# A hybrid decoder layer on one core: the input projection with seven doubled Strassen products, and attention in one small PSUM bank

## The chip, the cores and the metric

The kernel runs on one core of one Trainium2 chip. The metric is the device time of one execution in microseconds (us). The engines are named as in the profile: PE (TensorE, matmuls), PEld (its weight loads, which overlap PE), DVE (VectorE), ACT (ScalarE), POOL (GpSimd) and SP (SyncE, which issues most DMAs). PE writes its results into PSUM, which the kernel uses as eight banks of 128 x 512 float32.

## The reference

One layer on 512 tokens of width 2048, all in float32:

```python
h = rmsnorm(x, attn_norm_g)
proj = h @ w_in              # 2048 -> 9216: u, v_sgu, q, k, v_att (1024 each), g_a, g_b (2048 each)
u = gelu(u); v_sgu = rmsnorm(gelu(v_sgu), sgu_norm_g)          # 8 groups of 128
y_a = u * (tril(w_s) @ v_sgu + b_s)                            # in chunks of 128 tokens
q = rmsnorm(q, q_norm_g); k = rmsnorm(k, k_norm_g)             # 8 heads of 128
z = q @ k.T * scale                                            # strictly causal
w = exp(log_sigmoid(z) + reverse_cumsum(log_sigmoid(-z)) - log_sigmoid(-z))   # stick breaking
y_b = w @ v_att
x = x + (sigmoid(g_a) * (y_a @ w_up_a) + sigmoid(g_b) * (y_b @ w_up_b)) @ w_o
hid = rmsnorm(x, ffn_norm_g) @ w_ffn_in                        # 2 x 5632
x = x + (silu(gate) * up) @ w_ffn_out
x = x + sigmoid(rmsnorm(x, ple_norm_g) @ w_ple_gate) * (p @ w_ple)
```

## The kernel before

Activations lie transposed, features on the 128 partitions and the 512 tokens along the row. Every float32 product is made of three reduced ones: a number is split into a high part (`whi` for weights, made by ACT) and a low remainder (`wlo`, made by DVE), and high x high, high x low and low x high are added in a PSUM bank. On top of it lies a Strassen scheme: an output pair (256 features x 512 tokens, class `Pair`) is built from seven products of 128 x 128 blocks of weights with 256 columns of activations, instead of eight. DVE and ACT form the sums of weight blocks before (L382, splits L363 and L366), and the sums of products after (the generators `mix` and `mix_doubled`, in lines L757 and L760).

A product comes in two forms. In the **narrow** form (`mm3`, lines L296 to L298) it is three matmuls of 256 columns, and two products share a bank, one in each half. In the **doubled** form (L701) it is one matmul of 512 columns, high weights against the high and the low activations side by side, and one of 256 columns with the low weights. A doubled product needs a bank of its own, and the two halves of that bank are added later. The argument `doubled` of a pair says how many of its seven products take this form: 5 in the input projection, 7 in w_o, the feed-forward and its output.

The input projection has 36 pairs: q, k and v of round 0, some gates, q, k and v of round 1, and so on for four rounds of two heads each, then the gated branch (units s and u). Three pairs at the start are plain; the other 33 run over all 2048 inputs in four quarters of two weight blocks each, 14 products a quarter. Twice in a quarter `tick()` advances a clock and issues work that has come due: builds of operands, and the steps of the generators started with `beside`: flips (transposes) with the norms of q, k and v, attention, gating. A `yield n` in such a generator means "go on n ticks later". The order in which an engine gets its instructions follows the program, but a step of a generator may stand later among the products, and products of the next quarter may be drawn ahead; the chains made with `in_turn` and `mark` hold the weights and the mix in their order.

Eight PSUM banks are shared: six in the pool `psm` (tile `ps`) for products, two in the pool `psa` (tile `small`). With 5 doubled products a pair of the projection takes five banks and one for the two narrow products, so all of `psa` is for the steps beside it, and they take its two banks by turns: flips (L1055), scores (stage a, L1129), running sums (stage d, L1166 and L1167), the product with v (finish, L1181) and the gating (L1240). In pairs with 7 doubled products the seventh takes a bank of `psa`, by turns too.

Of the kernel before, what the change touches and what calls it, by code (L numbers as in the profile page):

```python
# [70 lines left out]
def hybrid_layer(  # L71
# [25 lines left out]
    psa = ctx.enter_context(tc.tile_pool(name="psa", bufs=2, space=PSUM))  # L97
# [85 lines left out]

    def bank():
        return psm.tile([P, T], F32, tag="ps", name=nm("ps"))
# [54 lines left out]
    class Staged:  # L240
# [23 lines left out]
        def get(self):  # L264
            while not self.done:
                self.advance()
            return self.result

# [373 lines left out]
    class Pair:  # L642
# [329 lines left out]
    class Norm:  # L972
# [17 lines left out]
        def steps(self):  # L990
            ps = small_bank()
            for t in range(NT):
                nc.tensor.matmul(ps[:, t : t + 1], self.acc.f(t * P, (t + 1) * P), ones[:, 0:1],
                                 start=True, stop=True)
            yield
            self.mean = consts.tile([P, NT], F32, name=nm("mean"))
            nc.vector.tensor_scalar(out=self.mean, in0=ps[:, :NT], scalar1=1.0 / D, scalar2=EPS,
                                    op0=ALU.mult, op1=ALU.add)
            self.cols = consts.tile([P, NT], F32, name=nm("cols"))
            nc.gpsimd.tensor_tensor(out=self.cols, in0=self.mean, in1=expo[:, :NT], op=ALU.pow)  # L1000
            for _ in range(3):
                yield
            ps = spread(self.cols)
# [99 lines left out]
    def v_prep(o, v):  # L1103
        for h in range(2):
            yield 2
            times(v[:, h * T : (h + 1) * T], flip(o[:, h * T : (h + 1) * T]), norm1.cols)

    def attention(rnd, kT, rk, v):
# [80 lines left out]
        blocks = [(h, j) for h in range(2) for j in range(NT - 1, -1, -1)]  # L1189
        stage_a(*blocks[0])  # L1190
        yield 1
        stage_m(*blocks[0])
        yield 1
        stage_a(*blocks[1])
        for i, (h, j) in enumerate(blocks):
            ahead = blocks[i + 1 : i + 3]
            if i == NT + 1:
                finish(0)
            stage_b(j)
            yield 1  # L1200
            stage_c(j)
# [9 lines left out]
        yield 1  # L1211
        finish(1)
# [4 lines left out]
    def sgu_v(rnd, o):  # L1217

        for h in range(2):
# [7 lines left out]
            yield 2  # L1227
# [8 lines left out]
            yield 2  # L1236
            mp = small_bank()
# [32 lines left out]
    def made():  # L1270
# [54 lines left out]
    for n, ((w, i), pr) in enumerate(zip(order, made())):  # L1325
# [10 lines left out]
        elif w == "k":  # L1336
            kT, rk = o, rms_tile()
            beside(k_prep(kT, rk))
            beside(attention(i, kT, rk, a_tile("v", 1024)), 6)
        elif w == "v":  # L1340
            beside(v_prep(o, a_tile("v", 1024)))
# [263 lines left out]
```

## Time and profile before

| | |
|---|---|
| median of 3 runs | 2657.65 us (2652.71 to 2658.19) |
| profiled execution | 2652.22 us; span 2650.5 us; TensorE clock 0.999 |
| PE, PEld busy | 2635.0 us (99%), 2301.7 us (87%) |
| DVE, ACT, POOL busy | 2255.1 us (85%), 1409.0 us (53%), 451.5 us (17%) |
| matmuls | 15202 |
| loads of the projection's weights (w_in) issued | 58.8 to 780.5 us; the last finish of attention (L1181) at 589 us |
| loads of w_ffn_in issued | 1152.9 to 1996.4 us |

The page of the profile gives, for each engine, busy time and number of instructions. A row of groups reads: line, engine, operation, output <- inputs, shapes, count, then busy time and mean duration in ns, then the idle time of the engine just before and what ended it. A row of the chain or of the timeline begins with the start in us from the span's start, and the length. Matmuls overlap in the pipeline: the chain shows what each adds, the timeline how long each is under way.

### The profile page before, as it was taken

Reading aid. Unit: us, or ns where it says so; the run is one execution under the profiler, and the core shown is the slowest. Engines: PE = TensorE matmul, PEld = TensorE weight load, DVE = VectorE, ACT = ScalarE, POOL = GpSimd, SP = SyncE. Lnnn points to the kernel's source line nnn. Section 1 sums busy time; section 2 is a strip of 40 time slices with the busy share of each in tenths; the row PEclk is TensorE's granted clock in tenths of the full one; section 3 lists DMA queues with packets and bytes.
Section 4 is the critical chain, followed back from the end, with each engine's and each line's share of the span. In section 5 each row is a group of like instructions: output and inputs, shape, how many; then the busy total and the mean of one; then the engine's idle time right before and its main releaser. Section 6 shows DMA issues by size and latency. Waiting matters only on the chain.

```text
span 2650.5 us, 42355 instructions
## 1 busy us (share of the span) xinstructions
PE 2635.0 (99%) x15202; PEld 2301.7 (87%) x15202; DVE 2255.1 (85%) x3856; ACT 1409.0 (53%) x2245; POOL 451.5 (17%) x559
## 2 busy tenths in 40 slices
PE   9999999999999999999999999999999999999999
PEld 7888888889998888888888888888888888889888
DVE  8687878787887558999888888888889989989898
ACT  7756565655554335466444444444445445455543
POOL 0222223232220001101111111111110211211010
PEclk9999999999999999999999999999999999999999
DMA  6777777677775669988888788888887989988794
GB/s 209 183 195 171 194 172 192 171 192 191 175 195 186 223 224 271 254 246 212 223 213 217 197 203 203 195 212 201 202 203 225 255 227 275 225 242 254 239 269 137
DMA packets 288130, 561.46 MB, mean 212 GB/s; under 512 B 26288, under 2 KB 133552, under 8 KB 287920
## 3 DMA queue, kind: packets, MB, share of 16 engines
q1 hardware_dynamic: 225856, 440.77, 50.6%
q0 software_dynamic: 61776, 117.47, 27.8%
q8 instruction: 119, 1.95, 0.3%
q14 instruction: 91, 0.75, 0.1%
q10 hardware_dynamic: 288, 0.52, 0.1%
HBM read 507.28 MB, written 51.38 MB: 211 GB/s over the span
## 4 chain that ended last, share of the span: by engine, by line
PE 94%; DVE 3%; ACT 1%; DMA 1%; issue 1%; SPq 0%; DVEq 0%; ACTq 0%
PE ps L701 56%; PE ps L298 9%; PE ps L297 9%; PE ps L296 9%; PE small L701 6%; DVE wlo L363 1%; PE small L1181 1%; PE small L1129 1%; PE small L1055 1%; DVE parts L287 1%; DVE wholes L534 0%; DVE wholes L382 0%; PE small L1240 0%; DMA wholes<-x 0%; DMA wholes<-w_ffn_out 0%
## 5 line engine op out<-in xcount | busy, mean ns | idle before, releaser
L701 PE MATMUL ps<-parts,whi 128*128 128x512 f32 x4390 | 1470.6, 398 | 1.9 <-DVE out L806 0.8
L366 ACT ACTIVATE whi<-wholes 128x512 fp32r<-128x512 f32 (+2 forms) x934 | 873.1, 948 | 759.4 <-DVE wholes L382 308.6
L363 DVE TENSOR_TENSOR wlo<-wholes,whi 128x512 fp32r<-128x512 f32 (+2 forms) x934 | 980.8, 1086 | 78.5 <-ACT whi L366 77.6
L701 PEld LDWEIGHTS ps<-parts,wlo 128*128 128x128 f32 x4390 | 823.9, 188 | 188.0 <-DVE wlo L363 2.5
L701 PE MATMUL ps<-parts,wlo 128*128 128x256 f32 x4390 | 868.4, 279 | 1.1 <-DVE wlo L363 1.1
L701 PEld LDWEIGHTS ps<-parts,whi 128*128 128x128 f32 x4390 | 707.2, 189 | 11.3 <-issue 3.1
L297 PE MATMUL ps<-parts,whi 128*128 128x256 f32 (+1 forms) x1622 | 538.4, 332 | 1.0 <-DVE parts L287 0.9
L298 PE MATMUL ps<-parts,wlo 128*128 128x256 f32 (+1 forms) x1622 | 538.3, 333 | 1.1 <-DVE wlo L363 1.1
L296 PE MATMUL ps<-parts,whi 128*128 128x256 f32 (+1 forms) x1612 | 532.5, 332 | 1.8 <-ACT parts L286 1.4
L382 DVE TENSOR_TENSOR wholes<-wholes 128x256 f32<-128x256 f32 x820 | 346.3, 422 | 15.8 <-DVE wlo L363 0.4
L760 DVE TENSOR_TENSOR out<-out,ps 128x256 f32<-128x256 f32 x525 | 216.8, 416 | 152.2 <-ACT out L757 152.0
L297 PEld LDWEIGHTS ps<-parts,whi 128*128 128x128 f32 x1622 | 305.9, 189 | 37.9 <-DVE parts L287 2.9
L298 PEld LDWEIGHTS ps<-parts,wlo 128*128 128x128 f32 x1622 | 306.2, 189 | 30.6 <-DVE wlo L363 1.5
L296 PEld LDWEIGHTS ps<-parts,whi 128*128 128x128 f32 x1612 | 303.5, 189 | 32.2 <-ACT parts L286 2.2
L370 POOL DMA_DIRECT2D wholes<-w_ffn_in x169 | 147.6, 873 | 704.2 <-DVE wholes L382 209.7
L370 POOL DMA_DIRECT2D wholes<-w_in x132 | 117.0, 888 | 543.1 <-DMA wholes<-w_in 112.3
L701 PE MATMUL small<-parts,whi 128*128 128x512 f32 x480 | 190.2, 397 | 0.0
L757 ACT ACTIVATE out<-ps 128x256 f32<-128x256 f32 x279 | 104.7, 385 | 57.0 <-PE ps L701 52.9
L287 DVE TENSOR_TENSOR parts<-wholes,parts 128x1024 fp32r<-128x1024 f32 (+3 forms) x139 | 124.0, 904 | 12.6 <-ACT parts L286 12.5
L286 ACT ACTIVATE parts<-wholes 128x1024 fp32r<-128x1024 f32 (+3 forms) x139 | 107.8, 797 | 46.5 <-DVE wholes L534 32.4
L370 POOL DMA_DIRECT2D wholes<-w_ffn_out x64 | 55.9, 873 | 356.0 <-DMA wholes<-w_ffn_out 84.7
L1428 ACT ACTIVATE out<-out 128x512 f32<-128x512 f32 x44 | 27.9, 633 | 156.2 <-DVE out L1427 156.2
(135 smaller groups left out, 1833.6 us busy)
## 6 DMA issues: line engine op xcount, KB each, us to landing
wholes<-w_ffn_in SPq DMA_DIRECT2D x169, 384.0 KB, 5.6
wholes<-w_in SPq DMA_DIRECT2D x132, 384.0 KB, 5.0
wholes<-w_ffn_in SPq DMA_DIRECT2D x169, 256.0 KB, 4.8
wholes<-w_ffn_in POOLq DMA_DIRECT2D x169, 256.0 KB, 5.4
wholes<-w_in SPq DMA_DIRECT2D x132, 256.0 KB, 4.1
wholes<-w_in POOLq DMA_DIRECT2D x132, 256.0 KB, 5.0
wholes<-w_ffn_out SPq DMA_DIRECT2D x64, 384.0 KB, 6.0
wholes<-x SPq DMA_DIRECT2D x46, 512.0 KB, 6.1
```

The costliest lines, as they stand in the source:

```text
L286: return (nc.scalar.activation(hi, src, AF.Copy), nc.vector.tensor_tensor(out=lo, in0=src, in1=hi.bitcast(F32), op=ALU.subtract))
L287: nc.vector.tensor_tensor(out=lo, in0=src, in1=hi.bitcast(F32), op=ALU.subtract))
L296: nc.tensor.matmul(ps, sh, mh, start=start, stop=False)
L297: nc.tensor.matmul(ps, sh, ml, start=False, stop=False)
L298: return nc.tensor.matmul(ps, sl, mh, start=False, stop=stop)
L363: in_turn(nc.vector.tensor_tensor(out=self.lo[:, blocks], in0=r, in1=h.bitcast(F32), op=ALU.subtract))
L366: in_turn(nc.scalar.activation(h, r, AF.Copy))
L370: nc.gpsimd.dma_start(out=raw[:, 3:5], in_=self.src[:, 1:3], accum_op=ALU.add)
L382: in_turn(nc.vector.tensor_tensor(out=o, in0=x, in1=y, op=ALU.add))
L701: m = nc.tensor.matmul(out, l, r, start=first and k == 0, stop=last and k == 1)
L757: in_turn(nc.scalar.activation(out, x, AF.Copy, scale=scale))
L760: in_turn(nc.vector.tensor_tensor(out=out, in0=x, in1=y, op=op))
```

## The change

The pairs of the input projection get `doubled=7`. Their seventh product takes a bank, so the pool `psa` now holds one bank called `last`, for the seventh product wherever a pair has one (in the pairs with both kinds of operands and 5 doubled products, for the bank called z), and one called `small` for all the steps beside. A new generator `turn(ticks)` lets a step wait until the ticks that the step before it took are over. `until_made` makes attention wait for q, k and v, which are now made at ticks that are not known beforehand; the sums, the finish and the scores, which were issued in one tick, are now in ticks of their own.

```diff
-    psa = ctx.enter_context(tc.tile_pool(name="psa", bufs=2, space=PSUM))
+    psa = ctx.enter_context(tc.tile_pool(name="psa", bufs=1, space=PSUM))
...
+    def last_bank():
+        return psa.tile([P, T], F32, tag="last", name=nm("last"))
...
+    taken = [0]
+
+    def turn(ticks):
+
+        while clock[0] < taken[0]:
+            yield 1
+        taken[0] = clock[0] + ticks
...
-                small = "z" if self.both and self.doubled else len(PRODUCTS) - 1
-                self.banks[name] = small_bank() if name == small else bank()
+                last = "z" if self.both and self.doubled else len(PRODUCTS) - 1
+                self.banks[name] = last_bank() if name == last else bank()
...
         def steps(self):
+            taken[0] = max(taken[0], clock[0] + 1)
             ps = small_bank()
...
         for h in range(2):
-            yield 2
+            yield 2 - h
+            yield from turn(2)
             ps = flip(o[:, h * T : (h + 1) * T])
...
             yield 2
+            yield from turn(1)
             if not h:
                 y_b[i] = take(1024)
             nc.scalar.activation(y_b[i].f(h * T, (h + 1) * T), flip(q.f()), AF.Copy,
                                  scale=gcol[:, g_q : g_q + 1])
             give(q)
-
-    def k_prep(o, rk):
+            made_up.add(("q", i, h))
+
+    made_up = set()
+
+    def until_made(*what):
+        while what not in made_up:
+            yield 1
...
-            yield 2
+            yield 2 - h
+            yield from turn(1)
             times(v[:, h * T : (h + 1) * T], flip(o[:, h * T : (h + 1) * T]), norm1.cols)
+        made_up.add(("v", i))
...
+        yield from until_made("k", rnd)
+        yield from until_made("q", rnd, 0)
+        yield from turn(1)
         stage_a(*blocks[0])
         yield 1
         stage_m(*blocks[0])
         yield 1
+        yield from turn(1)
         stage_a(*blocks[1])
         for i, (h, j) in enumerate(blocks):
             ahead = blocks[i + 1 : i + 3]
-            if i == NT + 1:
-                finish(0)
             stage_b(j)
             yield 1
+            if i == NT + 1:
+                yield from until_made("v", rnd)
+                yield from turn(1)
+                finish(0)
             stage_c(j)
             if ahead:
                 stage_m(*ahead[0])
             yield 1
             if not ahead:
                 yield 1
+            yield from turn(1)
             stage_d(h, j)
+            yield 1
             if ahead[1:]:
+                yield from until_made("q", rnd, ahead[1][0])
+                yield from turn(1)
                 stage_a(*ahead[1])
-            yield 1
         yield 1
+        yield from turn(1)
         finish(1)
...
             yield pair(xs, last=i == len(srcs) - 1, home=lambda: block(*order[i]),
-                       doubled=5)
+                       doubled=7)
```

The flips of k and the two uses of the gating get a `turn` in the same way.

What PE gets, in a quiet quarter of a pair of the gated branch. Before, the fifth product is doubled and the rest is narrow (`ps_631` holds both narrow products):

```order
L701 MATMUL ps_630_6215<-parts_73,whi1_77 128x512
L701 MATMUL ps_630_6215<-parts_73,wlo1_78 128x256 x2
L701 MATMUL ps_630_6215<-parts_73,whi1_77 128x512
L296 MATMUL ps_631_6220<-parts_73,whi1_77 128x256
L297 MATMUL ps_631_6220<-parts_73,whi1_77 128x256
L298 MATMUL ps_631_6220<-parts_73,wlo1_78 128x256
```

On PE after, in the first quarter of the next pair of that branch (lines are eleven higher; `ps_674` is the first product's bank, `ps_678`, `ps_679` and `last_680` those of the fifth, sixth and seventh):

```order
L712 MATMUL ps_678_5939<-parts_73,whi1_77 128x512
L712 MATMUL ps_674_5913<-parts_73,whi0_75 128x512
L712 MATMUL ps_674_5913<-parts_73,wlo0_76 128x256
L712 MATMUL ps_679_5944<-parts_73,whi1_77 128x512
L712 MATMUL ps_679_5944<-parts_73,wlo1_78 128x256 x2
L712 MATMUL ps_679_5944<-parts_73,whi1_77 128x512
L712 MATMUL last_680_5949<-parts_73,whi1_77 128x512
L712 MATMUL last_680_5949<-parts_73,wlo1_78 128x256 x2
```

Twelve narrow matmuls of a quarter have become eight of L712, in two banks; two matmuls of the next quarter (weights `whi0`, `wlo0`) have been drawn ahead of the sixth product. Pairs with seven doubled products elsewhere show the same at their start.

On PE before, sums and scores in an attention round, in two banks (`small_600`, `small_601`); the finish ahead of them stands nine products earlier:

```order
L297 MATMUL ps_599_5801<-parts_73,whi0_75 128x256
L298 MATMUL ps_599_5801<-parts_73,wlo0_76 128x256
L1166 MATMUL small_600_5814<-parts_73,tri1_133 128x256
L1167 MATMUL small_600_5814<-parts_73,tri1_133 128x256
L1129 MATMUL small_601_5821<-wholes_74 128x512
L701 MATMUL ps_593_5761<-parts_73,whi2_79 128x512
```

On PE after, the same three uses from the end of the finish (L1207) over the sums (L1192, L1193) to the scores (L1155), now all in the one bank:

```order
L1207 MATMUL small_645_5569<-wholes_74 128x128
L712 MATMUL ps_641_5527<-parts_73,whi1_77 128x512
L712 MATMUL ps_641_5527<-parts_73,wlo1_78 128x256 x2
L712 MATMUL ps_641_5527<-parts_73,whi1_77 128x512
L1192 MATMUL small_647_5596<-parts_73,tri1_133 128x256
L1193 MATMUL small_647_5596<-parts_73,tri1_133 128x256
L712 MATMUL last_642_5532<-parts_73,whi1_77 128x512
L712 MATMUL last_642_5532<-parts_73,wlo1_78 128x256 x2
L712 MATMUL last_642_5532<-parts_73,whi1_77 128x512
L712 MATMUL ps_634_5490<-parts_73,whi0_75 128x512
L712 MATMUL ps_634_5490<-parts_73,wlo0_76 128x256 x2
L1155 MATMUL small_649_5628<-wholes_74 128x512
```

The finish has moved to two products ahead of the sums, and the scores have moved from right behind the sums to where a product and two thirds lie between (seven matmuls).

On DVE before, the end of the mix of a pair (`p5` is a scratch tile, `wholes` and `out` hold the output):

```order
L760 TENSOR_TENSOR wholes_74<-wholes_74,p5_632_6322 128x2x256
L760 TENSOR_TENSOR wholes_74<-wholes_74,ps_630_6215 128x256
L760 TENSOR_TENSOR wholes_74<-ps_631_6220,wholes_74 128x512
L382 TENSOR_TENSOR wholes_74<-wholes_74 128x256
L1250 TENSOR_TENSOR wholes_74<-wholes_74 128x1024
```

On DVE after:

```order
L771 TENSOR_TENSOR wholes_74<-wholes_74,p5_681_6035 128x2x256
L771 TENSOR_TENSOR wholes_74<-wholes_74,ps_678_5939 128x256
L771 TENSOR_TENSOR wholes_74<-ps_679_5944,wholes_74 128x256
L771 TENSOR_TENSOR wholes_74<-last_680_5949,wholes_74 128x256
L771 TENSOR_TENSOR wholes_74<-wholes_74,ps_679_5944 128x256
L771 TENSOR_TENSOR wholes_74<-wholes_74,last_680_5949 128x256
L393 TENSOR_TENSOR wholes_74<-wholes_74 128x256
L1288 TENSOR_TENSOR wholes_74<-wholes_74 128x1024
```

One operation of 512 columns has become four of 256, two for each of the two new banks.

More of the change, by code (lines that the diff above doesn't have):

```diff
@@ L1002, in steps @@
                 yield
+            taken[0] = max(taken[0], clock[0] + 2)
             ps = spread(self.cols)
@@ L1095, in q_prep, with k_prep, v_prep @@
             give(q)
-    def k_prep(o, rk):
+            made_up.add(("q", i, h))
[3 more added lines that the diff above has]
+            yield 1
+    def k_prep(o, rk, i):
         for h in range(2):
-            yield 2
+            yield 2 - h
+            yield from turn(1)
             token_rms(flip(o[:, h * T : (h + 1) * T]), rk[:, NT * h : NT * (h + 1)])
         nc.scalar.activation(o, o, AF.Copy, scale=gcol[:, g_k : g_k + 1])
-    def v_prep(o, v):
+        made_up.add(("k", i))
+    def v_prep(o, v, i):
         for h in range(2):
-            yield 2
+            yield 2 - h
+            yield from turn(1)
             times(v[:, h * T : (h + 1) * T], flip(o[:, h * T : (h + 1) * T]), norm1.cols)
+        made_up.add(("v", i))
     def attention(rnd, kT, rk, v):
@@ L1206, in attention @@
                 yield 1
+            yield from turn(1)
             stage_d(h, j)
+            yield 1
             if ahead[1:]:
+                yield from until_made("q", rnd, ahead[1][0])
+                yield from turn(1)
                 stage_a(*ahead[1])
-            yield 1
         yield 1
+        yield from turn(1)
         finish(1)
@@ L1226, in sgu_v @@
             nc.sync.dma_start(out=bb, in_=b_s[g : g + 1, :].broadcast_to([P, P]))
-            yield 2
+            yield 2 - h
+            yield from turn(2)
             gv = a_tile(("l", "w0")[rnd % 2])
@@ L1236, in sgu_v @@
             yield 2
+            yield from turn(1)
             mp = small_bank()
@@ L1337, in hybrid_layer @@
             kT, rk = o, rms_tile()
-            beside(k_prep(kT, rk))
+            beside(k_prep(kT, rk, i))
             beside(attention(i, kT, rk, a_tile("v", 1024)), 6)
         elif w == "v":
-            beside(v_prep(o, a_tile("v", 1024)))
+            beside(v_prep(o, a_tile("v", 1024), i))
         elif w == "s":
```

## The prediction, made before the changed kernel ran

> **What bounds the kernel now.** I read the page first (busy shares, chain of waits), then the waits of TensorE (PE) alone, then the chain in a quiet stretch of the input projection beside one of the feed-forward stage, and last the timeline around the attention's banks.
>
> ```profile
> PE 2635.0 (99%) x15202; PEld 2301.7 (87%) x15202; DVE 2255.1 (85%) x3856; ACT 1409.0 (53%) x2245; POOL 451.5 (17%) x559
> PE 94%; DVE 3%; ACT 1%; DMA 1%; issue 1%; SPq 0%; DVEq 0%; ACTq 0%
> wholes<-w_in SPq DMA_DIRECT2D x132, 384.0 KB, 5.0
> ```
>
> PE is busy for 99% of the span and carries 94% of the chain, so an edit counts if it changes what PE streams or makes PE wait. The third row counts the work: 132 loads of weights, four to a pair of output tiles, are the 33 pairs that the change touches.
>
> The next answer is the waits of PE between 56 and 735 us, where the attention runs beside the projection; then four stretches of time (their length, then busy time and count of PE, PEld, DVE, ACT, POOL, then clock, DMA share, GB/s).
>
> ```profile
> PE small L1129 <- ACT wholes L1078: 1.2, 3, 0.5
> ```
> ```profile
> 56.00:735.00 679.00, 677.73 (x4283) 603.45 (x4282) 549.04 (x998) 421.48 (x890) 176.19 (x240) 1.00 0.73 183
> 273.70:293.50 19.80, 19.80 (x119) 16.93 (x118) 19.01 (x39) 14.50 (x30) 8.39 (x12) 1.00 0.74 199
> 610.10:629.90 19.80, 19.80 (x131) 17.99 (x131) 15.71 (x26) 10.96 (x14) 3.47 (x4) 1.00 0.77 189
> 1440.00:1459.80 19.80, 19.80 (x116) 17.28 (x115) 17.58 (x33) 9.64 (x14) 3.46 (x4) 1.00 0.79 200
> ```
>
> PE waits 1.2 us in 679: there is almost nothing to win from waits, and all that the two small banks do today is already hidden. DVE has room on the whole (549 of 679), but not in the middle of an attention round (19.01 of 19.80).
>
> **Part 1: products 5 and 6 doubled.** Here is the chain in a quiet pair of the input projection, then in a feed-forward pair, which already has seven doubled products (start, length, what).
>
> ```profile
> 601.51 3.51 PE ps L701 x20
> 605.02 0.12 PE ps L296
> 605.14 0.12 PE ps L297
> 605.26 0.12 PE ps L298
> ...
> 606.46 3.51 PE ps L701 x20
> ...
> 621.30 3.51 PE ps L701 x20
> ```
> ```profile
> 1464.37 4.19 PE ps L701 x24
> 1468.56 0.70 PE small L701 x4
> 1469.26 4.18 PE ps L701 x24
> ...
> 1483.90 0.24 PE ps L701
> ```
>
> A quarter pair of the projection is 20 matmuls for ten doubled products (3.51 us, 0.351 each) and twelve narrow ones for four products (605.02 to 606.46, 1.44 us, 0.36 each). Four quarters take 621.30 - 601.51 = 19.79 us. The feed-forward pair has the same 56 products, all doubled, and takes 1483.90 - 1464.37 = 19.53. The change makes the one into the other: 0.26 us a pair, 33 pairs, 8.6 us less. The low bound is the price of the products alone, 0.36 - 0.351 = 0.009 for 2 x 8 x 33 = 528 products, 4.8 us; I take the pair because it includes the passages between the kinds. So the instructions removed, 528 of 15202 or 3.5%, are worth only 0.3%: a wide matmul streams the columns of the two it replaces.
>
> [...]
>
> **Part 2: the mix on DVE.** One subtraction of 512 columns goes, four of 256 come. First the projection's end of a pair, then the feed-forward's:
>
> ```profile
> 603.62 0.68 DVE L760 TENSOR_TENSOR out<-ps,out 128x512 f32<-128x512 f32 x1
> 604.23 0.88 DVE L382 TENSOR_TENSOR wholes<-wholes 128x256 f32<-128x256 f32 x2
> ```
> ```profile
> 1442.12 0.42 DVE L760 TENSOR_TENSOR out<-ps,out 128x256 f32<-128x256 f32 x1
> 1442.45 0.41 DVE L760 TENSOR_TENSOR out<-small,out 128x256 f32<-128x256 f32 x1
> 1442.79 0.41 DVE L760 TENSOR_TENSOR out<-out,ps 128x256 f32<-128x256 f32 x1
> 1443.11 0.41 DVE L760 TENSOR_TENSOR out<-out,small 128x256 f32<-128x256 f32 x1
> 1443.44 0.42 DVE L382 TENSOR_TENSOR wholes<-wholes 128x256 f32<-128x256 f32 x1
> ```
>
> From start to next start the one takes 0.61 us, the four take 1443.44 - 1442.12 = 1.32: DVE gets 0.71 us more a pair, 23 us in all. In the quiet pair that is 16.4 of 19.5, less than the 17.58 that the feed-forward carries with no stall, so it costs nothing. In the worst pair of a round it is 19.01 + 0.71 = 19.7 against 19.5: DVE is full, and 0.2 us late with what follows. The cover is the room of the pairs beside it and the weights split ahead. I price it at 0; with that cover gone it is 0.2 to 0.7 us in perhaps two pairs of each of four rounds, 1.6 to 5.6 us. ScalarE's (ACT's) four copies a pair stay.
>
> **Part 3: one bank called last, also behind the attention.** The seventh product had two banks by turns in the feed-forward, w_o, w_ffn_out; now one. PE before wrote the next one while DVE still read the old one (1443.11 + 0.41 = 1443.52):
>
> ```profile
> 1443.28 0.40 PE L701 MATMUL small<-parts,whi 128*128 128x512 f32 x1
> 1443.63 0.39 PE L701 MATMUL ps<-parts,whi 128*128 128x512 f32 x1
> ```
>
> That can't be any more. But the order now puts two matmuls of the next quarter and the sixth product ahead of it, so that it would start near 1443.63 + 0.70 = 1444.33, 0.8 us after the read. I price it at 0; were DVE later by more than 0.8 us at every boundary, some 60 pairs would pay the excess.
>
> **Part 4: attention, flips and gating through one small bank.** This is the unknown, since nothing in the trace uses one bank for all of it. A round has 26 uses (8 flips, 8 scores, 8 sums, 2 finishes), four rounds 104. Each use must now wait until ACT or DVE has read the one before. With PE first in line for 99% of the span, each such wait is lost time; and behind the waiting matmul stands every product of the projection. The timeline before, at the finish of the first half of the third round (L1181 is the finish and L1183 reads it; L1167 ends the sums and L1173 reads them):
>
> ```profile
> 422.85 0.27 DVE L1173 TENSOR_TENSOR wholes<-wholes,small 128x128 f32<-128x128 f32 x1
> 423.26 2.39 PE L1181 MATMUL small<-wholes 128*128 128x512 f32 x8
> 425.69 0.60 ACT L1183 ACTIVATE wholes<-small 128x512 f32<-128x512 f32 x1 [1.65 <-PE small L1181]
> 428.80 0.28 PE L1167 MATMUL small<-parts,tri 128*128 128x256 f32 x1
> 429.86 2.27 DVE L363 TENSOR_TENSOR wlo<-wholes,whi 128x1280 fp32r<-128x1280 f32 x2
> 432.45 0.40 DVE L1173 TENSOR_TENSOR wholes<-wholes,small 128x256 f32<-128x256 f32 x1
> ```
>
> At 423.26 PE writes a bank whose last read ended at 422.85 + 0.27 = 423.12: the order brings the use 0.14 us after the release, and PE has no idle time there. That is the row nearest to the new situation. The order of the changed kernel shows how many products now lie between two uses. At this same place they are two (0.70 us) from the finish to the sums, whose reader needs 0.04 + 0.60 us; and 1.17 us from the sums to the scores. Before, the sums ended near 429.08 and were read by 432.85, 3.77 us later, since a split of weights of 2.27 us stood ahead on DVE. If DVE is free, the read is done 0.8 us after the sums.
>
> ```profile
> L1078 ACT ACTIVATE wholes<-small,cols 128x128 f32<-128x128 f32 x32 | 9.5, 369 | 3.2 <-PE small L1055 3.2
> L1131 ACT ACTIVATE wholes<-small,rr 128x512 f32<-128x512 f32 x8 | 5.5, 689 | 5.3 <-PE small L1129 4.6 <-DVE wholes L382 0.7
> L1132 ACT ACTIVATE wholes<-small,rr 128x512 f32<-128x512 f32 x8 | 5.5, 684 | 0.9 <-DVE wholes L534 0.9
> ```
>
> The other short distances of a round, by the order: 4 products (1.40 us) after a flip of v, whose readers need 4 x 0.369 = 1.48; 4 products after scores of 512, whose readers need 0.689 + 0.684 = 1.37; and 1.63 and 1.51 us after two other sums. The rest have 2.1 to 12.8 us.
>
> Low end: every use arrives after its release, 0 us; or the 1.2 us that PE waits today goes too, since scores now start only once q is made. High end: the three short distances after sums (1.63, 1.51, 1.17) meet a read 3.8 us late, 7.1 us a round, 28 us in four rounds. I take 0.5 us a round (0.1 to 0.2 for each flip, score and finish above, the sums mostly in time), 2.0 us, near the low end, because PE came 0.14 us behind a release without waiting. The flips and their readers move later by a tick or two; nothing queues behind that, since by the order the second finish of a round lies 12.8 us of PE work ahead of the next round's first flip.
>
> **The sum.** -8.6 (products) + 0 (mix) + 0 (last bank) + 2.0 (small bank) = -6.6 us. The profiled execution took 2652.22 us (span 2650.5 and 1.7 around it), so 2645.6. It stands 5.4 us under the median of the three runs, 2657.65 (2652.71 to 2658.19); from that median the sum gives 2651.0. Two of three runs lie at the upper value, so I say 2650.
>
> **Rivals.** One: a product costs its columns and nothing else. All products stream 768 columns before and after, so the gain is about 0, and 2.0 of waits stand against it: 2654 from the own time. The row of 0.36 against 0.351 and the 19.53 us pair speak against it. [...]
>
> Two, the same time in another way: the gain is given back in waits of 3.3 to 13.9 us, 0.8 to 3.5 us a round, at the short distances or at the full pairs of DVE: 2646.9 to 2657.5 from the own time, 2652 in the middle. The 19.01 of 19.80 speaks for it, that PE today waits for no read of a bank against it.
>
> Three, slower: reads of the sums stay 3.8 us late, because they still stand behind weight splits on DVE, which now also carries 0.71 us more a pair. PE then stops in each round at the three short distances, 28 us in all, less 8.6: 2671. It decides from 3.5 us of waits a round (8.6 + 5.3 over four rounds). For it speaks the 3.77 us above, and that the order of the changed kernel still has two splits ahead of such a read on DVE; against it, that those splits may be over by then, since scores and sums come later than before.
>
> **How the numbers follow.** About 0.2% (5.3 us) is what a measurement of this kernel tells from no change. The sum's case (net gain 5.3 to 9.8 us) gets 0.57; rival one 0.06 and rival two 0.24, together 0.30 for the same; rival three 0.13. So faster 0.57, same 0.30, slower 0.13. The low end is the full 8.6 and the 1.2 from the own time, 2642.4, with a little for the runs' spread: 2641. The high end is a median of runs unchanged and a small loss of 3 us: 2661. Under the sum's case alone it is 2642 to 2652.
>
> **What would show it.** Right: PE's narrow products L296 to L298 of the projection gone, quiet pairs at 19.53 us in place of 19.79, PE at 14674 matmuls, feed-forward pairs still at 19.53. The small bank: PE's waits between 56 and 730 us name ACT and DVE readers of it and sum to about 2 us (high: 28). DVE in the worst 19.5 us stretch full, with no PE wait on wlo. Wrong: quiet pairs above 19.7 us (rival one), PE waits over 3.5 us a round behind the sums' readers or at a pair's start (rivals two, three), or feed-forward pairs above 19.53 (part 3).

## Result and the profile after

The changed kernel takes 2673.95 us, the median of 6 runs (2668.51 to 2678.19), beside 2655.47 for the kernel before on the same chip (6 runs). The ratio is 1.0069, interval 1.0055 to 1.0083: 0.7% slower, where 2650 us was forecast. The profiled execution took 2676.11 us, its span is 2674.4 us, against 2650.5 before.

The page of the changed kernel, busy shares and the chain of waits (share of the span by engine):

```profile
PE 2639.3 (99%) x14674; PEld 2274.5 (85%) x14674; DVE 2278.2 (85%) x3955; ACT 1407.6 (53%) x2245; POOL 440.0 (16%) x559
PE 79%; DVE 11%; DMA 4%; issue 2%; ACT 2%; POOL 1%; DVEq 0%; POOLq 0%; SPq 0%; ACTq 0%
```

The 528 matmuls are gone, as announced, and DVE has 23 us more. PE still reads 99% busy, which tells nothing of the loss. The second row does: PE's share of the chain fell from 94% to 79%, and DVE, DMA, ACT and POOL carry parts of it now.

PE's waits between 56 and 735 us (what PE was to run, for whom it waited; total, times, longest), where before showed 1.2 us for the scores:

```profile
PE small L1278 <- ACT wholes L1091: 6.5, 3, 2.9
PE small L1192 <- ACT wholes L1158: 4.0, 1, 4.0
PE small L1192 <- ACT parts L1182: 1.0, 3, 0.3
PE small L1207 <- ACT wholes L1158: 0.7, 2, 0.5
PE ps L712 <- DVE wlo L374: 0.2, 1, 0.2
PE ps L712 <- DVE p L771: 0.2, 1, 0.2
```

Together they are 12.6 us, where about 2 were forecast. The first four rows are matmuls into the small bank, and all four wait for ACT: L1278 is the gating product, L1192 the first matmul of a sum, L1207 the finish; L1091 scales the gating input by its power, L1158 reads scores, L1182 makes the high half of the sums' operand. DVE's splits of weights (wlo), where the prediction looked, stand in one row of 0.2 us. The window ends ahead of one gating product; with it the first row is 9.5 us in 4 waits, the longest 3.0.

The chain in the last pair of the projection (start, length, what):

```profile
788.24 0.70 PE last L712 x4
788.94 4.54 PE ps L712 x26
...
807.76 0.70 PE last L712 x4
```

From one seventh product to that of the next pair it is 807.76 - 788.24 = 19.52 us, against 19.79 before: a quiet pair does win its 0.27 us.

Where the 23.9 us of the two spans lie is seen from the start of one pair to the start of a later one (worked out from PE's matmuls in both traces; 33 pairs, and what is before and behind them):

| stretch | before, us | after, us | difference |
|---|---|---|---|
| ahead of the pairs | 84.5 | 85.2 | +0.7 |
| 7 pairs with round 0 | 156.77 | 162.19 | +5.4 |
| 6 + 6 pairs with rounds 1, 2 | 268.33 | 268.94 | +0.6 |
| 5 pairs with round 3 | 111.50 | 112.87 | +1.4 |
| 7 pairs with gating | 149.27 | 159.57 | +10.3 |
| last 2 pairs | 39.57 | 39.04 | -0.5 |
| behind the projection | 1840.6 | 1846.6 | +6.0 |

So there are three losses: the gating, the rounds, the start of the up-projection. In the places shown below, something in an engine's queue waits for a transfer or a buffer, and work that PE needs stands behind it.

**The gating.** Rows of the timeline of after, on POOL, ACT and PE (start, length, engine, line; in brackets the idle time before and what ended it):

```profile
645.89 0.89 POOL L381 DMA_DIRECT2D wholes<-w_in  x1 [4.56 <-DMA wholes<-w_in]
646.46 1.39 POOL L965 TENSOR_TENSOR rr<-ms,expo 128x4 f32<-128x4 f32 x1
647.89 1.14 ACT L1091 ACTIVATE wholes<-small,rr 128x128 f32<-128x128 f32 x4 [2.80 <-POOL rr L965]
649.08 1.16 PE L1278 MATMUL small<-wholes 128*128 128x128 f32 x8 [2.88 <-ACT wholes L1091]
```

L381 is POOL's issue of the transfer that adds one block of weights onto another. Here the load below it landed at 645.23, and the issue began at 645.89, after POOL had stood idle for 4.56 us; the power of 128x4 numbers (L965), next in POOL's queue, begins at 646.46 although DVE had its operand ready at 642.08, ACT's scaling waits 2.80 us for the power, and the gating product, with all of PE behind it, 2.88 us for the scaling. The same place before:

```profile
633.79 0.89 POOL L370 DMA_DIRECT2D wholes<-w_in  x1 [2.17 <-DVE ms L1231]
634.37 1.39 POOL L954 TENSOR_TENSOR rr<-ms,expo 128x4 f32<-128x4 f32 x1
635.79 1.14 ACT L1078 ACTIVATE wholes<-small,rr 128x128 f32<-128x128 f32 x4 [1.67 <-POOL rr L954]
636.40 1.08 PE L1240 MATMUL small<-wholes 128*128 128x128 f32 x8
```

The order was the same and PE did not wait, but the slack was small: the product began 0.61 us after the scaling did, while it was still under way. In this place the load was asked for at 639.10 and landed at 645.23 (6.1 us); before it was asked for at 630.25 and landed at 633.13 (2.9 us). In both kernels a split of weights on DVE releases the load (L374, begun at 637.59; before L363, at 628.74).

**Round 0.** The same on POOL's masks, after:

```profile
153.47 0.89 POOL L381 DMA_DIRECT2D wholes<-w_in  x1 [4.39 <-issue]
154.06 0.62 POOL L1168 TENSOR_SCALAR_AFFINE_SELECT wholes<-wholes 128x128 f32<-128x128 f32 x1
154.74 0.20 POOL L1176 MEMSET wholes<- 1x128 f32 x1
154.97 0.63 ACT L1182 ACTIVATE parts<-wholes 128x512 fp32r<-128x512 f32 x1 [4.08 <-POOL wholes L1176]
156.17 0.36 ACT L1158 ACTIVATE wholes<-small,rr 128x128 f32<-128x128 f32 x1
156.57 0.79 PE L1192 MATMUL small<-parts,tri 128*128 128x512 f32 x1 [3.99 <-ACT wholes L1158]
```

The bracket of the first row says issue, which names no releaser; the load that this issue adds onto landed at 152.43. The mask waits behind the issue on POOL, the copy L1182 for the mask on ACT, the read of the next scores (L1158) behind that copy, and PE for the read, since there is one bank: 3.99 us.

**The start of the up-projection**, ACT and PE after:

```profile
833.25 1.06 ACT L377 ACTIVATE whi<-wholes 128x1024 fp32r<-128x1024 f32 x1 [3.00 <-PE ps L308]
834.22 1.04 ACT L297 ACTIVATE parts<-wholes 128x1024 fp32r<-128x1024 f32 x1
835.31 0.73 PE L307 MATMUL ps<-parts,whi 128*128 128x512 f32 x2 [1.42 <-ACT parts L297]
```

ACT holds a copy of weights that waits for PE to release the place it writes, and the operand y that PE needs stands behind it. A second stop of 1.30 us at 843.34 follows a load of y that SP issues at 836.73, behind two loads of w_up_a; before, that load went ahead of them.

### The profile page after: what moved, and what is told of

Same layout as the page of the kernel before. It is cut to its first block, busy times and chain, and to the rows that moved or that the text cites. A ratio compares the mean times of both kernels' runs of the same rounds, so it can differ in the third digit from the quotient of the medians.

```text
span 2674.4 us, 41430 instructions
## 1 busy us (share of the span) xinstructions
PE 2639.3 (99%) x14674; PEld 2274.5 (85%) x14674; DVE 2278.2 (85%) x3955; ACT 1407.6 (53%) x2245; POOL 440.0 (16%) x559
## 4 chain that ended last, share of the span: by engine, by line
PE 79%; DVE 11%; DMA 4%; issue 2%; ACT 2%; POOL 1%; DVEq 0%; POOLq 0%; SPq 0%; ACTq 0%
PE ps L712 51%; PE last L712 8%; PE ps L309 6%; PE ps L308 6%; PE ps L307 6%; DVE wlo L374 4%; DVE out L771 2%; DMA wholes<-w_ffn_out 1%; DVE wholes L393 1%; DVE wholes L545 1%; DVE parts L298 1%; DMA wholes<-w_in 1%; PE small L1207 1%; DMA wholes<-x 1%; ACT whi L377 1%
## 5 line engine op out<-in xcount | busy, mean ns | idle before, releaser
L712 PE MATMUL ps<-parts,whi 128*128 128x512 f32 x4654 | 1544.0, 398 | 2.3 <-DVE out L817 0.9
L712 PEld LDWEIGHTS ps<-parts,wlo 128*128 128x128 f32 x4654 | 874.7, 188 | 198.6 <-DVE wlo L374 3.1
L374 DVE TENSOR_TENSOR wlo<-wholes,whi 128x512 fp32r<-128x512 f32 (+2 forms) x934 | 981.1, 1086 | 68.0 <-ACT whi L377 65.7
L712 PE MATMUL ps<-parts,wlo 128*128 128x256 f32 x4654 | 931.9, 279 | 1.3 <-DVE wlo L374 1.3
L712 PEld LDWEIGHTS ps<-parts,whi 128*128 128x128 f32 x4654 | 745.8, 189 | 17.9 <-issue 4.2
L308 PE MATMUL ps<-parts,whi 128*128 128x512 f32 (+1 forms) x1094 | 390.1, 357 | 0.9 <-DVE parts L298 0.7
L309 PE MATMUL ps<-parts,wlo 128*128 128x512 f32 (+1 forms) x1094 | 388.3, 357 | 2.0 <-DVE wlo L374 2.0
L307 PE MATMUL ps<-parts,whi 128*128 128x512 f32 (+1 forms) x1084 | 383.2, 357 | 4.4 <-ACT parts L297 4.0
L712 PE MATMUL last<-parts,whi 128*128 128x512 f32 x744 | 295.1, 397 | 0.0
L381 POOL DMA_DIRECT2D wholes<-w_ffn_in x169 | 149.3, 883 | 701.4 <-DVE wholes L393 213.1
L308 PEld LDWEIGHTS ps<-parts,whi 128*128 128x128 f32 x1094 | 206.8, 189 | 32.3 <-DVE parts L298 2.7
L307 PEld LDWEIGHTS ps<-parts,whi 128*128 128x128 f32 x1084 | 203.8, 189 | 35.0 <-ACT parts L297 5.5
L309 PEld LDWEIGHTS ps<-parts,wlo 128*128 128x128 f32 x1094 | 206.9, 189 | 31.1 <-DVE wlo L374 2.6
L381 POOL DMA_DIRECT2D wholes<-w_in x132 | 117.3, 891 | 517.8 <-DMA wholes<-w_in 161.7
L712 PEld LDWEIGHTS last<-parts,wlo 128*128 128x128 f32 x744 | 139.8, 188 | 33.6 <-issue 0.7
L712 PE MATMUL last<-parts,wlo 128*128 128x256 f32 x744 | 148.6, 280 | 0.0
L712 PEld LDWEIGHTS last<-parts,whi 128*128 128x128 f32 x744 | 140.3, 189 | 0.8 <-issue 0.7
```

Source lines behind the costliest of these rows:

```text
L307: nc.tensor.matmul(ps, sh, mh, start=start, stop=False)
L308: nc.tensor.matmul(ps, sh, ml, start=False, stop=False)
L309: return nc.tensor.matmul(ps, sl, mh, start=False, stop=stop)
L374: in_turn(nc.vector.tensor_tensor(out=self.lo[:, blocks], in0=r, in1=h.bitcast(F32), op=ALU.subtract))
L381: nc.gpsimd.dma_start(out=raw[:, 3:5], in_=self.src[:, 1:3], accum_op=ALU.add)
L712: m = nc.tensor.matmul(out, l, r, start=first and k == 0, stop=last and k == 1)
```

## Experiments

Two theories stand against each other. By the first, POOL's queue is the cause: what makes a weights' load later (a longer mix, other ticks) makes masks and powers late. By the second, the distances in the one bank are too short, or DVE is simply full. All ratios are against the kernel before on the same chip, whose median was 2654.1 to 2655.5 us in the four groups of runs. A ratio can differ a little from that of the two medians, so the differences in us below, taken between medians and partly between groups, are good to 1 to 2 us.

**e1, the bank alone.**

```diff
-                       doubled=7)
+                       doubled=5)
```

> The changed kernel with 5 doubled products in the projection again: one small bank and the ticks alone. The profile of the changed kernel lost about 8 us in round 0 and 2 us in each of three more rounds at the small bank, about 12 us in the gated branch (PE waits for the normalized v, L1278 behind L1091), and 4 us at the start of the next stage. Theory A (one bank and the ticks make all of it): 2655 + 26 = 2681 us. Theory B (the bank makes the rounds' losses, the doubling the rest): about 2655 + 12 = 2667 us, no wait of PE at the gating product above 0.5 us. Theory C (the doubling makes all, through the longer mix on DVE): 2655 us.

2674.75 us (ratio 1.0071, 1.0058 to 1.0084), as slow as the whole change. That lies between theories A and B: the bank and the ticks alone make the rounds' losses, and one gating wait of 2.3 us too. PE's longest item of waits:

```profile
PE small L1192 <- ACT wholes L1158: 9.5, 4, 2.7
```

It is the wait of round 0 above, now once in each round: in all four places ACT's copy (L1182) waits for POOL. In two of them the issue is not the whole of POOL's lateness: the mask L1168 itself takes 1.31 us (at 286.29) and 2.25 us (at 422.61), against 0.62 in round 0, while DVE splits weights beside it. In the traces of before and after, all masks that take over 1.2 us (9 and 8) lie beside such a split; those with no work of DVE beside them (4 and 6) take 0.29 to 0.33 us. No run parts this from the wait for landings, since taking the masks off POOL ends both. The 33 pairs take 746.7 us (+21.3); behind them the time is that of before (1839.9).

**e2, the longer mix alone**: the kernel before with two additions of 256 columns into scratch in every mix, 0.67 us of DVE a pair.

```diff
                     tt(o[:, :T], self.at("y"), o[:, :T], sub)
+                    tt(s5, s5, s5, add)
+                    tt(s5, s5, s5, add)
```

> The kernel before with two more operations of 256 columns at the end of each mix of the projection, on a scratch tile: 0.67 us more of DVE a pair, nothing else. Theory C or B (the longer mix delays the splits, so the loads, so what stands behind them on POOL): PE waits of 2 to 3 us at the gating products appear, 2655 + 8 to 12 = 2663 to 2667 us. Theory A: 2655 us, and no new wait of PE.

2666.28 us (1.0034, 1.0022 to 1.0046), 11 us lost by the medians and 9 by the ratio, with the old bank, ticks and products:

```profile
PE small L1242 <- ACT wholes L1080: 6.9, 3, 2.8
```

L1242 is the gating product here. Of the 13.5 us that the pairs lose, 12.0 lie in the seven gating pairs (161.31 against 149.27). So the doubled mix is not free.

**e3, the first gating product two ticks later.**

```diff
-            yield 2
+            yield 4 - 2 * h
```

> The changed kernel with the first gating product of each unit two ticks (4.9 us) later. If PE waits there because its operand is late (power on POOL behind an issue of weights that waits for a landing), the four waits of 1.9 to 3.3 us and the low clock behind them go: 2674 - 12 = 2662 us. If they only show a delay that lies elsewhere (DMA too slow for the pair), another wait takes their place: 2672 to 2674 us.

2671.82 us (1.0059, 1.0046 to 1.0071): 2 us less, within the spread of the change's runs. The gating pairs go from 159.57 to 156.0, but e7 below, with the gating as it was, has 153.15, so one trace of each does not tell the two apart. The waits for the power sink from 9.5 to 2.8 us in all, and small waits of products for the mix (1.8 us) come in. More distance mends little, and this run alone would not show what makes the operand late.

**e4, no power**: the changed kernel, with the power of the gating norm left out (a copy on DVE in its place).

```diff
-            rr = power(ssq, NT)
+            rr = rms_tile()[:, :NT]
+            nc.vector.tensor_scalar(out=rr, in0=ssq, scalar1=1.0, scalar2=EPS,
+                                    op0=ALU.mult, op1=ALU.add)
```

> The changed kernel with the power of the gated branch's norm left out (a copy on DVE in its place, so the norm's factor is not computed): POOL has nothing of that chain. If the power waits on POOL behind the issue of weights, PE's waits at the gating products go, as with the product two ticks later: 2662 us. If the operand is late for ACT's or DVE's sake, they stay: 2672 to 2674 us.

2661.25 us (1.0023, 1.0014 to 1.0032): 12.7 us less than the change, and the gating pairs at 147.65, below before. So the gating loss hangs on one operation of 128x4 on POOL.

**e5, the columns alone**: the kernel before with seven doubled products, the seventh in the same two small banks as the attention.

```diff
-                       doubled=5)
+                       doubled=7)
```

> The kernel before with all seven products of the input projection doubled and nothing else: two small banks by turns, shared by the attention and the seventh product, and the attention's old ticks. Queue theory (the longer mix makes the chain of DVE split, weights' load, accumulation on POOL, power on POOL late; the streaming gain is real): 8.6 us gained in the products, 8 to 13 us lost at the gating products, as in the run with the longer mix: 2650 to 2662, near 2656, the waits at the gating products with the rr or wholes made behind them. Rival (the one bank is the whole cause, doubling is harmless): 2645 to 2649, no gating waits over 1 us.

2674.02 us (1.0074, 1.0062 to 1.0087): worse than I expected, and as slow as the whole change, without its bank. The waits, then one of them through the engines:

```profile
PE ps L701 <- DVE p L760: 6.4, 4, 1.7
PE small L1240 <- ACT wholes L1078: 6.3, 3, 2.9
```
```profile
449.36 0.89 POOL L370 DMA_DIRECT2D wholes<-w_in  x1 [3.58 <-DMA wholes<-w_in]
450.62 0.20 POOL L1150 MEMSET wholes<- 1x128 f32 x1
450.85 0.63 ACT L1156 ACTIVATE parts<-wholes 128x512 fp32r<-128x512 f32 x1 [3.16 <-POOL wholes L1150]
452.20 0.42 DVE L760 TENSOR_TENSOR out<-out,ps 128x256 f32<-128x256 f32 x1 [3.43 <-ACT out L757]
455.34 0.80 PE L701 MATMUL ps<-parts,whi 128*128 128x512 f32 x1 [1.69 <-DVE p L760]
```

The same issue on POOL, the same mask, the same copy on ACT. Only the end differs: behind ACT's copy stand the copies of the mix (L757), DVE waits 3.43 us for them and then has a split of weights to do (2.09 us from 452.54) ahead of the read that frees the bank, and PE waits for a product's bank. With one small bank the late copy meets the scores, with two it meets the mix.

**e6, no masks**: the changed kernel, with the attention's masks and the zeroing of a row left out.

> The changed kernel without the four operations a block that POOL does for the attention's masks: both masks and the zeroing of the row are left out (scores unmasked), the copy of the row goes to DVE. Queue theory (POOL's masks stand behind the weights' accumulation, ACT's read of the next scores behind the copy that needs them, PE behind the one bank): the wait of some 4 us in the first round goes, and the waits of 0.3 to 0.6 us at the sums in the others: 8 to 14 us less than the changed kernel, 2660 to 2666, while the gating waits of about 10 us stay. Rival (the distances in the one bank themselves are too short, POOL only happens to be late): within 3 us of the changed kernel, 2671 to 2675.

2663.57 us (1.0030, 1.0020 to 1.0041), 10.4 us less than the change. The first 24 pairs take 533.5 us instead of 544.0 (before 536.6), the waits at the sums are gone and the gating keeps its own:

```profile
PE small L1268 <- ACT wholes L1091: 9.4, 4, 3.1
```

**e7, the last two pairs with five.**

```diff
-                       doubled=7)
+                       doubled=5 if i >= len(srcs) - 2 else 7)
```

> The changed kernel with the last two pairs of the projection back at five doubled products. If the late start of the up-projection (3.6 us, PE waiting for the operands of y at 835 us) comes from the doubled last pairs, as the run with five everywhere suggests: 2669 to 2672, that wait gone. If it comes from elsewhere (the gating's end or the loads): 2674 to 2676.

2667.84 us (1.0047, 1.0035 to 1.0059). Behind the projection it is 1839.1 us instead of 1846.6; its order has the operand y ahead of that copy of weights on ACT. The rest of the profile's gain lies in gating pairs (153.15), which this edit doesn't touch: that loss varies by some 6 us from one execution to another.

**e8, the longer mix without the power**: e2 with the edit of e4, the power left out.

> The kernel before with the longer mix (0.67 us of DVE a pair more) and the power of the gating norm not computed (a copy on DVE in its place). Queue theory (in the kernel before too the longer mix costs only because the power stands on POOL behind the weights' accumulation): the 11 us of the longer mix go, 2653 to 2658. Rival (DVE itself is late for the gating products, or for the products' operands): 2663 to 2667 as with the power.

2656.52 us (1.0006, 0.9997 to 1.0014). Of the 11 us that the longer mix cost, 9.8 are gone (7.4 of 9 by the ratios). DVE's time itself was nearly covered, as the prediction said; the queue behind it was not.

**e9, nothing left out, POOL out of the way**: the changed kernel with the masks on DVE, the power as Ln and Exp on ACT with their table loaded ahead, and e7's edit.

```diff
-            nc.gpsimd.affine_select(out=s[:, :P], in_=s[:, :P], pattern=[[1, P]],
-                                    compare_op=ALU.is_gt, fill=0.0, base=0,
-                                    channel_multiplier=-1)
+            tt(s[:, :P], s[:, :P], a_tile("mask", P), ALU.min)
...
-            nc.gpsimd.affine_select(out=w[:, :P], in_=w[:, :P], pattern=[[1, P]],
-                                    compare_op=ALU.is_gt, fill=MASKED, base=0,
-                                    channel_multiplier=-1)
+            nc.vector.scalar_tensor_tensor(out=w[:, :P], in0=a_tile("mask", P), scalar=MASKED,
+                                           in1=w[:, :P], op0=ALU.add, op1=ALU.min)
...
-            rr = power(ssq, NT)
+            rr = rms_tile()[:, :NT]
+            nc.scalar.activation(ssq, ssq, AF.Ln)
+            nc.scalar.activation(rr, ssq, AF.Exp, scale=-0.5)
```

> The changed kernel with nothing left out and three things taken out of POOL's and ACT's way: the attention's masks on DVE (a minimum with a constant mask, a second minimum, a memset of one row, in place of POOL's selects), the power of the gating norm as Ln and Exp on ACT with its table loaded ahead, and five doubled products in the last two pairs. Queue theory: the three gains measured apart (12.7 without the power, 10.4 without the masks, 6.1 for the last pairs) add up, less what the masks cost DVE: 2645 to 2653, so at or below the kernel before. Rival (the waits move to the next reader when POOL is taken out, since the one bank has no slack): 2658 to 2670.

2653.52 us (0.9992, 0.9983 to 1.0001): 20.4 us less than the change. The longest wait left in the projection is at the one bank, the scores for DVE's read of a sum, some 1.1 us a round:

```profile
PE small L1158 <- DVE wholes L1197: 4.5, 4, 1.4
```

**e10, the same with the masks on POOL.**

> The same with the masks left on POOL: the power of the gating norm on ACT and five doubled products in the last two pairs. Queue theory: 12.7 and 6.1 less than the changed kernel, 2653 to 2659, with the 4 us wait of the first round and the small waits at the sums still there. Rival (Ln, Exp and two table loads on ACT make the gating factor as late as POOL did): 2664 to 2670, gating waits still 5 us or more.

2658.30 us (1.0009, 1.0000 to 1.0018). The masks are worth 4.8 us of e9, less than the 10.4 of leaving them out: now DVE has to do them, and the 4.5 us of waits above, which e6 doesn't have, are about the difference.

**e11 and e12, controls without the bank**: the kernel before with masks on DVE and power on ACT, and the same with seven doubled products.

> The kernel before with the masks on DVE and the power of the gating norm on ACT, as a control. Before has 1.2 us of waits in this stretch, so nothing is to be won: 2652 to 2657. If the masks on DVE cost what a longer mix costs: up to 2662.

2651.89 us (0.9987, 0.9979 to 0.9996).

> The same as the control, with all seven products doubled: two small banks by turns, the old ticks, masks on DVE, the power on ACT. Queue theory: of the 2674 of the doubled kernel with two banks the gating waits go (7 to 10 us), the waits of the products for the mix's reads (6 us) stay, since the seventh product still shares the banks with the attention: 2660 to 2667. Rival (those waits too came from late masks or power): 2647 to 2654, and the small bank would not have been needed.

2652.11 us (0.9989, 0.9980 to 0.9998). I had expected the waits for the mix to stay; they went as well, 22 us in all. So the small bank was not needed for the doubled products, POOL's work was their only price of any size. And the products win nothing net: the round-0 pairs of e12 take 159.1 us against 156.5 in e11. PE's waits there name 0.7 us for ACT's read of scores, 0.6 for the mix on DVE and 0.3 at a flip; the waits don't name the rest of the 2.6.

**e13, the bank alone, POOL out of the way; e14, seven everywhere, POOL out of the way.**

> One small bank and the ticks, five doubled products everywhere, masks on DVE and the power on ACT: against the control (two small banks, 2651.9) it prices the one bank alone with POOL out of its way. If the one bank has its own price (the wait of the scores for DVE's read of the sums, about 1.2 us in each round of the kernel with both parts): 4 to 7 us, 2655 to 2660. Rival (all of the 19.6 us of the bank alone came from POOL's queue): 2650 to 2654.

2652.77 us (0.9994, 0.9985 to 1.0003), 0.9 above the control e11, or 1.7 when each is set against the kernel before on its own chip; the 33 pairs of the traces differ by 1.1. That is the rival's case: the one bank is nearly free. PE has no wait of the scores for a sum here, so that wait in e9 needs the doubled products as well.

> The changed kernel with masks on DVE and the power on ACT, seven doubled products in all pairs, the last two as well. If the late start of the up-projection belongs to the doubled last pairs and not to POOL: 2657 to 2661, with PE waiting for the operands of y again. Rival (it followed from the late gating): 2651 to 2655.

2658.64 us (1.0014, 1.0005 to 1.0023), 5.1 above e9, and behind the projection 1846.3 against 1841.2 us. In this bank arrangement the late start belongs to the doubled last pairs, not to POOL. PE's waits for that operand over the whole run, 2.7 us of them at this start:

```profile
PE ps L307 <- ACT parts L297: 4.3, 4, 1.4
```

Which version is best? e11, e12, e9 and e13 lie within 2 us of each other and at most 0.13% under the kernel before, less than the 0.2% that the prediction took as telling from no change (the intervals of e11 and e12 end just under 1). None is a faster kernel worth the name.

## Why the prediction was wrong, step by step

**Part 1, -8.6 us: right in kind, too large.** The quiet pair was read rightly (19.79 to 19.52), but I carried it to pairs that hold a round. Summing, over six pairs of a round, the time from the end of each matmul to the end of the next for the products alone, gives 118.57 us before and 117.68 after, and 118.58 against 117.65 in e11 and e12: 0.15 us a pair. With 24 such pairs, 0.22 in each of the seven gating pairs (138.32 to 136.75 from e11 to e12) and 0.27 in the last two it is 3.6 + 1.5 + 0.5 = 5.6 us. The low bound of 4.8, from the products without the passages, was the nearer row. And a round keeps little of it: as whole pairs, the six of round 1 take 133.67 us in e11 and 133.59 in e12, because attention's matmuls between the products take 0.9 us more. Rival one (columns only) falls in the quiet pairs.

**Part 2, 0: this step failed.** I asked whether DVE's own time was covered, and it nearly is (e8). I didn't ask what DVE's work releases. In the place of the gating shown above, a split frees a landing place, the load into it is issued then (639.10), the accumulation on POOL waits for the landing (645.23), and the power waits behind it (646.46); in round 0 a mask waits so (landing 152.43, mask 154.06). In the pairs of round 1 a load is asked for ahead of the first product of its quarter, in the kernel before by 29.1 us and in e2 by 28.3 (means of 24 loads). Alone the longer mix costs 11 us (e2), beyond the 1.6 to 5.6 that I gave for a lost cover, since that bound priced DVE late by itself. The loads stood in my working only as a count of 132, not as something that is made later.

**Part 3, 0: right.** The pairs of w_o and the feed-forward still take 19.52 us, from the first of them in w_o to the end of the last it is 984.2 us before and 984.1 after, and the page has no idle time of PE ahead of the 744 wide matmuls with the high weights into `last`.

**Part 4, +2.0: near the price of the bank with POOL out of the way, wrong as the price of the step.** By itself the bank then costs 0.9 us (e13), and with the doubled products the waits at it are 4.5 us (e9). But I priced its readers as if each came right after PE, or 3.8 us late behind splits on DVE. The readers that are late stand on ACT behind a copy that needs POOL's mask or behind POOL's power, and POOL's queue was not in the working at all. With the masks on POOL the bank costs 19.6 us (e1). The uses that I listed left the gating out, which lost most.

The two costs don't add: 19.6 for the bank (e1), 19.9 for the columns (e5), 18.5 for both. Either makes the chain late that goes load, issue on POOL, mask or power, copy on ACT. It had little slack, as 1.2 us of waits in 679 could not tell: a wait of zero is no measure of the distance to a wait.

**Not in the prediction: the start of the up-projection**, +6.0 us, of which PE's waits name 3.4. With doubled last pairs in this bank arrangement ACT's order puts a copy of weights ahead of the operand y (after, e14); e7 has neither that order nor the loss. e5 doubles the last pairs too and loses 1.4 us only (1841.9), so the order that the two edits make together matters. More of it the runs don't show.

**The rivals.** Rival three gave 2671 us, near the measured value, but by another mechanism: it put the stop at the sums behind DVE's splits of weights ahead of the sums' reads, 28 us in four rounds, and no long wait names those reads. That its time came near is luck. The splits do play a part that it did not describe, beside POOL's masks (e1) and ahead of the mix (e5). Rival two allowed for 13.9 us of waits at most. Summed again with what was measured: the products -5.6; the gating pairs lost 10.3 although they won 1.5 in products, so 11.8 in waits and in the low clock behind one of them (9.5 of it waits; the clock was 0.50 from 716 to 718 us); the rounds 7.4 and 3.6, so 11.0, likewise; the start of the up-projection 6.0, ahead of the pairs 0.7. That is 23.9, as between the spans; it adds up because the waits are taken as what is left.

## What to carry to other kernels

In the places shown here an instruction that waited for a transfer (POOL, 4.56 us) or for a buffer (ACT, 3.00 us) was a gate for what stood behind it in its engine's queue, however small. Before an edit that makes any producer later, follow each short operation on the path of the bounding engine back through the queues of all engines, and ask what stands ahead of it there and for what that waits. And read slack from how early an operand is made, not from the absence of a wait.

## What the hardware showed unexpectedly

The granted clock (the column behind POOL) falls after some of these waits. Four stretches of after:

```profile
156.00:158.00 2.00, 1.43 (x4) 1.26 (x5) 0.32 (x1) 2.00 (x6) 0.00 (x0) 0.55 1.06 211
158.00:160.00 2.00, 2.00 (x9) 1.74 (x8) 1.89 (x6) 0.08 (x1) 1.21 (x3) 0.60 0.52 195
648.00:650.00 2.00, 0.92 (x9) 0.92 (x9) 0.67 (x2) 1.58 (x6) 0.93 (x1) 1.00 0.62 110
716.00:718.00 2.00, 2.00 (x10) 1.90 (x9) 0.75 (x1) 0.58 (x1) 0.38 (x1) 0.50 0.78 96
```

After the wait of 3.99 us it was 0.55 and 0.60, after one of 2.06 us (715.47) 0.50, after the ones of 2.88 us at 649 and 2.98 us at 762 it stayed at 1.00. So the wait of 2.06 us cost about as much again: the gating pair with it took 25.23 us, and 21.33 in e4 without it. Why the clock fell after this one and not after the longer ones at 649 and 762 us, the runs don't tell.

The other surprise is the landing of the same kind of load, 2.9 us before and 6.1 after at the same place in the program. The loads did not slow on the whole: by the pages the median of the 132 is 4.1 us before and 3.8 after. While this one was under way the DMA engines were 0.88 and 0.87 busy (640 to 642 and 642 to 644 us), and before, at the same place, 0.52 and 0.93 (630 to 632 and 632 to 634). Why more was under way just then, the runs don't tell.

A third is POOL's mask of 128x128, which takes 0.29 to 0.33 us with no work of DVE beside it (10 masks of before and after), and beside DVE's split of weights up to 2.95 us before and 2.88 after.
